# Attention of a two-block model: two heads at a time, matmuls in a fixed order

## The chip, the cores and the metric

The kernel runs on one core of a Trainium2 chip. The metric is the device time of one execution in microseconds. A core has a matrix engine (TensorE; its weight loads are listed apart, as PEld), VectorE (DVE), ScalarE (ACT), GpSimd (POOL) and a queue from which SyncE (SP) issues most loads. Matmul results land in PSUM, eight banks of 128 x 512 fp32 numbers; VectorE and ScalarE copy them on.

## What is computed

Two model blocks one after the other, 1024 tokens of width 1024. The change touches the attention of the second block only: two attentions of eight heads of width 64, cut into query blocks of 128.

```python
def forgetting_attention(q, k, v, log_f):          # "fox": own keys and values per head
    ...
        s = jnp.einsum('bqhd,bkhd->bhqk', q[:, start:end], k[:, :end], ...) * scale
        s = s + Ft[:, :, start:end, None] - Ft[:, :, None, :end]
        s = jnp.where(tk <= tq, s, -jnp.inf)
        p = jax.nn.softmax(s, axis=-1)
        outs.append(jnp.einsum('bhqk,bkhd->bqhd', p.astype(v.dtype), v[:, :end]))

def dsa_attention(q, k, v, qi, ki, wi):            # "dsa": one key and value head for all eight
    ...                                            # top-k choice of keys (here: an additive bias)
        s = jnp.einsum('bqhd,bqkd->bhqk', q[:, start:end], kg, ...) * scale
        p = jax.nn.softmax(s, axis=-1)
        outs.append(jnp.einsum('bhqk,bqkd->bqhd', p.astype(vg.dtype), vg))
```

## The kernel before

The program is written with tiles from pools; a planner orders each engine's instructions at build time by dependencies and modelled times, and each engine then runs its list in that order. `attention` (from L1530) comes after the projections of the second block and before `merge`, which multiplies the two attentions' outputs with their projection weights (L1715 loads them, L1726 to L1728 are its matmuls).

For a query block i (0 to 7) and a head, i+1 blocks of 128 keys take part, n = 128 (i+1) columns. `probs` (L1559) makes the scores: for each 512 columns a bank `pS` gets two matmuls (L1567 and L1570, fp32r, at least 256 columns wide), and in fox the last bank a third between them that adds the causal mask (L1569, bf16). VectorE adds the bias and keeps a running minimum (L1572), ScalarE takes the exponential and its row sum (L1574), both into the tile `S`. TensorE then transposes S block by block into a PSUM slot `pT` of up to four blocks (two such slots; L1624 in fox, L1657 in dsa), and `evac` (L1552) copies the slot to the tile `PT`, by ScalarE and VectorE in turn (L1555, L1557). The products with the values (L1629, L1661) accumulate over key blocks in the bank `po`: fp32 with 64 value columns as weights, the output in 64 of the 128 PSUM rows; each product is two records in the trace. After four query blocks (fox) or eight heads (dsa) `normalise` (L1577) inverts the row sums, spreads them by four matmuls (L1586) into a `pT` slot and scales `po`.

Fox runs over four pairs of heads (`hp2`), inside over the query blocks; a pair's two heads are in rows 0 to 63 and 64 to 127 of `po`, and the value products of the two heads take turns (L1627 to L1630). Its keys, queries and values are loaded per pair into one of two pools (`kps`), the row of forget sums `fr` into the first of them alone (L1598). Dsa (L1636 on) runs over the query blocks, inside over the eight heads, one after the other; heads 0 to 3 go to rows 0 to 63, heads 4 to 7 to rows 64 to 127. It has a pool of its own, `kp`, for its keys and two tiles of queries. Nothing ties TensorE to the written order: the planner mixes the kinds of matmul of different heads as they become ready.

Of the kernel before, what the change touches and what calls it, by code (L numbers as in the profile page):

```python
# [8 lines left out]
F32 = mybir.dt.float32  # L9
F32R = mybir.dt.float32r  # L10
# [3 lines left out]
AF = mybir.ActivationFunctionType  # L14
ALU = mybir.AluOpType
# [4 lines left out]
P = 128  # L20
D = 1024
NT = 8
# [1504 lines left out]
        self.es_h.close()  # L1527


def attention(B):  # L1530

    tc, dbg = B.tc, B.dbg
# [9 lines left out]
    with ExitStack() as e:  # L1542
        sp = e.enter_context(tc.tile_pool(name="b2s", bufs=3, reuse_waits="tile"))
        wk = e.enter_context(tc.tile_pool(name="b2ak", bufs=2, reuse_waits="tile"))
        kps = [e.enter_context(tc.tile_pool(name=f"b2k{j}", bufs=1, reuse_waits="tile")) for j in range(2)]
        kp = e.enter_context(tc.tile_pool(name="b2kd", bufs=2, reuse_waits="tile"))
        pss = e.enter_context(tc.tile_pool(name="b2pss", bufs=4, reuse_waits="tile", space=PSUM))
        pst = e.enter_context(tc.tile_pool(name="b2pst", bufs=2, reuse_waits="tile", space=PSUM))
        pso = e.enter_context(tc.tile_pool(name="b2pso", bufs=1, reuse_waits="tile", space=PSUM))
# [2 lines left out]
        def evac(dst, src):  # L1552
            flip[0] ^= 1
            if flip[0]:
                nc.scalar.copy(dst, src)  # L1555
            else:
                nc.vector.tensor_copy(dst, src)  # L1557

        def probs(q1, k1, k2, bias_ap, n, nm, diag, lsum):  # L1559

            S = sp.tile([P, 1024], F32, name=f"S{nm}", tag="S")
            mn = 3.0e38
            for lo in range(0, n, 512):
                pS = pss.tile([P, 512], F32, name=f"pS{nm}{lo}", tag="pS")
                w = min(512, n - lo)
                wm = max(256, w)
                nc.tensor.matmul(pS[:, :wm], q1, k1[:, lo:lo + wm], start=True, stop=False)  # L1567
                if diag and lo + 512 >= n:
                    nc.tensor.matmul(pS[:, w - P:w], identb, causb, start=False, stop=False)  # L1569
                nc.tensor.matmul(pS[:, :wm], q1, k2[:, lo:lo + wm], start=False, stop=True)  # L1570
                m = sp.tile([P, 1], F32, name=f"mn{nm}{lo}", tag="mn", bufs=8)
                nc.vector.tensor_tensor_reduce(S[:, lo:lo + w], pS[:, :w], bias_ap[:, lo:lo + w], 1.0, mn, ALU.add, ALU.min, m)  # L1572
                mn = m
            nc.scalar.activation(S[:, :n], S[:, :n], AF.Exp, bias=mn, scale=-1.0, accum_out=lsum)  # L1574
            return S

        def normalise(po, lsum, nm, cs, dh, dl):  # L1577

            rl = wk.tile([P, 2, 4], F32, name=f"rl{nm}", tag="rl")
            nc.vector.reciprocal(rl, lsum)  # L1580
            pr = pst.tile([P, 512], F32, name=f"prl{nm}", tag="pT")
            for j in range(4):
                rb = wk.tile([P, 2, 64], F32, name=f"rb{nm}{j}", tag="rlb", bufs=4)
                nc.vector.tensor_tensor(out=rb, in0=ones.rearrange("p (a b) -> p a b", a=2),
                                        in1=rl[:, :, j:j + 1].to_broadcast([P, 2, 64]), op=ALU.mult)
                nc.tensor.matmul(pr[:, j * P:(j + 1) * P], rb.rearrange("p a b -> p (a b)"), ident, start=True, stop=True)  # L1586
            rr = wk.tile([P, 512], F32, name=f"rr{nm}", tag="rr")
            nc.scalar.copy(rr, pr)
            nc.vector.tensor_tensor(out=rr, in0=rr, in1=po, op=ALU.mult)
            rv = rr.rearrange("p (a b) -> p a b", a=4)  # L1590
            nc.scalar.copy(dh, rv)
            nc.vector.tensor_tensor(out=dl, in0=rv, in1=dh.bitcast(F32), op=ALU.subtract)

        for hp2 in range(4):
            q1, k1, k2 = (kps[hp2 % 2].tile([P, 2, NT, P], F32R, name=f"{n}{hp2}", tag=n) for n in ("fq", "fk1", "fk2"))
            vt = kps[hp2 % 2].tile([P, NT, P], F32, name=f"fv{hp2}", tag="fvt")  # L1598
            fr = kps[0].tile([P, 2, 1024], F32, name=f"fr{hp2}", tag="fr")
            for half in range(2):  # L1600
                hs = slice(4 * half, 4 * half + 4)
                for dst, n in ((k1, "fk1"), (q1, "fq1"), (k2, "fk2")):
                    nc.sync.dma_start(dst[:, :, hs, :].bitcast(F32), st_d[n][:, 2 * hp2:2 * hp2 + 2, hs, :])
                if half == 0:
                    for q in range(2):
                        nc.sync.dma_start(fr[:, q, :], ft_d[2 * hp2 + q:2 * hp2 + q + 1, :].broadcast_to([P, 1024]))
                    nc.sync.dma_start(vt, fv_d[:, :, P * hp2:P * hp2 + P])
            for half in range(2):
                po = pso.tile([P, 512], F32, name=f"po{hp2}{half}", tag="po", bufs=2)
                ls = wk.tile([P, 2, 4], F32, name=f"ls{hp2}{half}", tag="ls")  # L1610
                for ii in range(4):
                    i = 4 * half + ii
                    n = (i + 1) * P
                    pts = []
                    for q in range(2):
                        nm = f"f{hp2}{i}{q}"
                        S = probs(q1[:, q, i, :], k1[:, q].rearrange("p t c -> p (t c)"),
                                  k2[:, q].rearrange("p t c -> p (t c)"), fr[:, q, :n], n, nm, True, ls[:, q, ii:ii + 1])
                        pT = sp.tile([P, 8, P], F32, name=f"PT{nm}", tag="PT", bufs=6)
                        for k0 in range(0, i + 1, 4):  # L1620
                            m = min(4, i + 1 - k0)
                            pp = pst.tile([P, 512], F32, name=f"pT{nm}{k0}", tag="pT")
                            for kk_ in range(m):
                                nc.tensor.transpose(pp[:, kk_ * P:(kk_ + 1) * P], S[:, (k0 + kk_) * P:(k0 + kk_ + 1) * P], ident)  # L1624
                            evac(pT[:, k0:k0 + m, :].rearrange("p a b -> p (a b)"), pp[:, :m * P])
                        pts.append(pT)
                    for kt in range(i + 1):  # L1627
                        for q in range(2):
                            nc.tensor.matmul(po[64 * q:64 * q + 64, ii * P:(ii + 1) * P], vt[:, kt, 64 * q:64 * q + 64],  # L1629
                                             pts[q][:, kt, :], start=(kt == 0), stop=(kt == i))  # L1630
                hs = slice(512 * half, 512 * half + 512)
                normalise(po, ls, f"f{hp2}{half}", hs, ofh[:, hp2, hs].rearrange("p (a b) -> p a b", a=4),
                          ofl[:, hp2, hs].rearrange("p (a b) -> p a b", a=4))


        dk1 = kp.tile([P, NT, P], F32R, name="dk1", bufs=1)  # L1636
        dk2 = kp.tile([P, NT, P], F32R, name="dk2", bufs=1)
        nc.sync.dma_start(dk1.bitcast(F32), dk_d[0])
        nc.sync.dma_start(dk2.bitcast(F32), dk_d[1])
        dk1 = dk1.rearrange("p t c -> p (t c)")  # L1640
        dk2 = dk2.rearrange("p t c -> p (t c)")
        for i in range(NT):
            n = (i + 1) * P
            q1 = kp.tile([P, 8, P], F32R, name=f"dq1_{i}", tag="dq1")
            nc.sync.dma_start(q1.bitcast(F32), dq_d[i])
            po = pso.tile([P, 512], F32, name=f"pod{i}", tag="po", bufs=2)
            ls = wk.tile([P, 2, 4], F32, name=f"lsd{i}", tag="ls")
            S = [None] * 8
            for h in range(8):
                S[h] = probs(  # L1650
                    q1[:, h, :], dk1, dk2, bias[i], n, f"d{i}{h}", False, ls[:, h // 4, h % 4:h % 4 + 1])
                pT = sp.tile([P, 8, P], F32, name=f"PTd{i}{h}", tag="PT", bufs=6)
                for k0 in range(0, i + 1, 4):
                    m = min(4, i + 1 - k0)
                    pp = pst.tile([P, 512], F32, name=f"pTd{i}{h}{k0}", tag="pT")
                    for kk_ in range(m):
                        nc.tensor.transpose(pp[:, kk_ * P:(kk_ + 1) * P], S[h][:, (k0 + kk_) * P:(k0 + kk_ + 1) * P], ident)  # L1657
                    evac(pT[:, k0:k0 + m, :].rearrange("p a b -> p (a b)"), pp[:, :m * P])
                q = h // 4
                for kt in range(i + 1):  # L1660
                    nc.tensor.matmul(po[64 * q:64 * q + 64, (h % 4) * P:(h % 4 + 1) * P], dvt[:, kt, :], pT[:, kt, :],  # L1661
                                     start=(kt == 0), stop=(kt == i))
            ts_ = slice(i * P, (i + 1) * P)
            normalise(po, ls, f"d{i}", None, odh[:, :, ts_], odl[:, :, ts_])
    B.es_a.close()
    B.of, B.od = (ofh, ofl), (odh, odl)
    if dbg and "of" in dbg:
# [586 lines left out]
```

## Time and profile before

| | us |
|---|---|
| median of three runs | 2946.06 (2944.88 to 2956.12) |
| the profiled execution | 2949.89 |
| its span, first to last instruction | 2948.1 |
| busy in the span: TensorE, weight loads | 2686.4 (91%), 2119.9 (72%) |
| busy: VectorE, ScalarE, GpSimd | 2128.3 (72%), 1484.9 (50%), 596.0 (20%) |
| mean granted clock of TensorE | 0.964 |

A busy share is the part of the span in which an engine has a record open; records of neighbouring matmuls overlap, so how fast matmuls follow each other is read from their starts. The granted clock is 1.00 at 2.4 GHz and 0.50 at 1.2 GHz; a stretch with both shows a mean.

### The profile page before, as it was taken

The numbers are of one execution on the slowest core, as the hardware profiler recorded it, in microseconds if no ns is written. First come the engines' busy times: TensorE is split into PE (matmuls) and PEld (weight loads), VectorE is DVE, ScalarE is ACT, GpSimd is POOL, SyncE is SP. The second block draws the span as 40 slices with busy tenths as digits, with TensorE's granted clock in tenths as the row PEclk, the third lists the DMA queues.
The fourth block names the chain that finished last, engine by engine and source line by source line (L and its number), as shares of the span: only waits on it lengthen the run. The fifth ranks groups of instructions, "written<-read, shape, count | busy, mean of one in ns | idle before, by whom it ended". The sixth has DMA issues, their size and how long they took to land. (4 is left out here: it accounts for less than half of the span.)

```text
span 2948.1 us, 39530 instructions
## 1 busy us (share of the span) xinstructions
PE 2686.4 (91%) x14016; PEld 2119.9 (72%) x14016; DVE 2128.3 (72%) x3664; ACT 1484.9 (50%) x2402; POOL 596.0 (20%) x449
## 2 busy tenths in 40 slices
PE   5999998999978897879999999999998799999997
PEld 2767776777757675658778777787777687777775
DVE  6776768876876567686676736654456899999996
ACT  4433334554532325557667535653122577777774
POOL 2000003333353214221222100000234212111112
PEclk9999999999989998899999999999999899999998
DMA  5255445654545232201322553002346799999995
GB/s 221 80 215 214 163 148 186 214 191 161 192 157 181 90 109 97 69 29 61 117 91 100 172 205 110 23 23 79 107 163 213 269 383 373 371 372 365 377 368 177
DMA packets 214180, 533.09 MB, mean 181 GB/s; under 512 B 25478, under 2 KB 70918, under 8 KB 209884
## 3 DMA queue, kind: packets, MB, share of 16 engines
q1 hardware_dynamic: 144768, 411.98, 39.3%
q10 hardware_dynamic: 57548, 84.99, 8.1%
q0 software_dynamic: 11664, 33.57, 4.6%
q8 instruction: 111, 1.82, 0.3%
q14 instruction: 89, 0.73, 0.1%
HBM read 449.25 MB, written 90.11 MB: 183 GB/s over the span
## 5 line engine op out<-in xcount | busy, mean ns | idle before, releaser
L2060 DVE TENSOR_TENSOR wh<-we,wh 128x1024 fp32r<-128x1024 f32 x390 | 456.3, 1219 | 15.5 <-ACT wh L2057 7.6
L2057 ACT CAST wh<-we 128x1024 fp32r<-128x1024 f32 x396 | 396.7, 1052 | 83.4 <-PE pye L2119 24.2
L450 DVE SCALAR_TENSOR_TENSOR acc<-img,cvw,acc 128x945 f32<-128x945 f32 (+2 forms) x160 | 193.1, 1219 | 53.8 <-ACT acc L441 51.8
L2096 PE MATMUL pae<-wh,xle 128*128 128x512 f32 x528 | 207.5, 394 | 5.9 <-DVE xle L2081 5.9
L2094 PE MATMUL pae<-wh,xhe 128*128 128x512 f32 x528 | 210.6, 399 | 2.2 <-ACT xhe L2080 2.2
L2095 PE MATMUL pae<-wh,xhe 128*128 128x512 f32 x528 | 209.9, 398 | 0.2 <-DVE wh L2060 0.2
L775 POOL TENSOR_TENSOR H<-H,expT 128x384 f32<-128x384 f32 x56 | 59.2, 1058 | 440.8 <-DMA H<-hs 349.7
L2117 PE MATMUL pye<-wh,ghe 128*128 128x512 f32 x264 | 107.4, 407 | 21.8 <-ACT ghe L2109 21.8
L2071 POOL DMA_INDIRECT xg<-h_d,gidx x33 | 35.9, 1089 | 448.5 <-PE pxe L2077 431.4
L2096 PEld LDWEIGHTS pae<-wh,xle 128*128 128x128 f32 x528 | 99.8, 189 | 27.0 <-DVE xle L2081 6.7
L2094 PEld LDWEIGHTS pae<-wh,xhe 128*128 128x128 f32 x528 | 100.0, 189 | 23.2 <-ACT xhe L2080 2.8
L2095 PEld LDWEIGHTS pae<-wh,xhe 128*128 128x128 f32 x528 | 100.0, 189 | 21.5 <-DVE wh L2060 1.4
L351 PE MATMUL pxz<-hTh,w_h 128*128 128x512 f32 x320 | 110.6, 413 | 3.0 <-ACT oz L705 2.4
L351 PE MATMUL pxc<-hTh,w_h 128*128 128x512 f32 x320 | 106.9, 408 | 5.1 <-ACT acc L441 5.1
L351 PE MATMUL pxz<-hTh,w_l 128*128 128x512 f32 x320 | 109.5, 412 | 0.0
L351 PE MATMUL pxz<-hTl,w_h 128*128 128x512 f32 x320 | 106.5, 407 | 0.0
L1751 POOL TENSOR_TENSOR sgl<-sgl 128x512 f32<-128x512 f32 x15 | 19.4, 1293 | 429.5 <-DMA wra<-in_w_pf 364.0
L768 POOL TENSOR_TENSOR xs<-xs,er 128x384 f32<-128x384 f32 x64 | 73.1, 1144 | 157.5 <-DVE er L766 140.5
L2119 PE MATMUL pye<-wh,gle 128*128 128x512 f32 x264 | 104.6, 396 | 0.1
L2118 PE MATMUL pye<-wh,ghe 128*128 128x512 f32 x264 | 103.4, 392 | 0.0
L1208 PE MATMUL ppg<-hg,h2Th 128*128 128x512 f32 x256 | 102.0, 400 | 0.6 <-ACT re L1360 0.6
L351 PE MATMUL pxc<-hTl,w_h 128*128 128x512 f32 x320 | 102.3, 397 | 0.0
(911 smaller groups left out, 7688.9 us busy)
## 6 DMA issues: line engine op xcount, KB each, us to landing
we<-in_w_ex SPq DMA_DIRECT2D x396, 512.0 KB
ad_w<-in_ada_w SPq DMA_DIRECT2D x24, 1024.0 KB
wr<-in_w_in SPq DMA_DIRECT2D x40, 512.0 KB
er<-ep_d SPq DMA_DIRECT2D x128, 96.0 KB
rbw<-pr_d SPq DMA_DIRECT2D x32, 384.0 KB
pf<-pr_d SPq DMA_DIRECT2D x32, 384.0 KB
xbc<-acc ACTq DMA_DIRECT2D x20, 512.0 KB
wada<-in_w_ada SPq DMA_DIRECT2D x8, 1024.0 KB
```

Of the source, the lines that this page charges most:

```text
L351: nc.tensor.matmul(px[j], wt[:, k, :mc], ht[:, k, 512 * j:512 * j + 512], start=(k == 0 and n == 0), stop=(k == KD - 1 and n == 2))
L450: nc.vector.scalar_tensor_tensor(o, img[:, r0 + dy:r1 + dy, c0 + dx:c1_ + dx], cvw[:, m, tap:tap + 1], o, op0=ALU.mult, op1=ALU.add)
L768: nc.gpsimd.tensor_tensor(out=y, in0=y, in1=er.rearrange("p (j t) -> p j t", j=3), op=ALU.add)
L1208: nc.tensor.matmul(pp, hTh[t][:, k, :], h, start=(k == 0), stop=False)
L2057: last["h"] = nc.scalar.copy(h, raw)
L2060: eng.tensor_tensor(out=l, in0=raw, in1=h.bitcast(F32), op=ALU.subtract)
L2094: nc.tensor.matmul(pa, xh[:, kk, :], h[:, cs], start=(kk == 0), stop=False)
L2095: nc.tensor.matmul(pa, xh[:, kk, :], l[:, cs], start=False, stop=False)
L2096: last["mm"] = nc.tensor.matmul(pa, xl[:, kk, :], h[:, cs], start=False, stop=(kk == KD - 1))
L2117: nc.tensor.matmul(o, gh[:, kk, :], h[:, cs], start=(kk == 0), stop=False)
L2118: nc.tensor.matmul(o, gh[:, kk, :], l[:, cs], start=False, stop=False)
L2119: nc.tensor.matmul(o, gl_[:, kk, :], h[:, cs], start=False, stop=(kk == 3))
```

## The change

Fox and dsa become generators of units: two heads and a query block. In dsa a unit holds heads j and j+4. For each unit all score matmuls of both heads are written first, the causal masks after them as the last matmul of their group. A step then writes the scores of one unit, the transposes of the unit two before it (`TLAG`) and the products of the unit before that: first up to four blocks of each head are transposed, into the two `pT` slots, then comes the first half of the products, in turns between the heads, then the other transposes and the rest of the products. `keep_in_program_order` ties these matmuls to this order on TensorE; VectorE, ScalarE and the loads are planned as before. `normalise` is split: the spreading matmuls come at the end of a later step. Buffers: S has six instead of three, PT five instead of six, the minimum twelve instead of eight, the row sums three instead of two; `fr` is in both pools; `kp` is gone, dsa's keys and queries lie in tiles of fox's size in `kps`, the queries two blocks to a tile. The copies of a unit's first head go to ScalarE and those of the second to VectorE, since the turns now go by head.

```diff
+TLAG = 2
+SBUFS = 6
...
-        kp = e.enter_context(tc.tile_pool(name="b2kd", bufs=2, reuse_waits="tile"))
...
-        def probs(q1, k1, k2, bias_ap, n, nm, diag, lsum):
...
+        queued = tc.keep_in_program_order
+
+        def scores(heads, n, nm, diag):
+
+            ps, res = [], []
+            for q, (q1, k1, k2, _, _) in enumerate(heads):
+                for lo in range(0, n, 512):
+                    pS = pss.tile([P, 512], F32, name=f"pS{nm}{q}{lo}", tag="pS")
+                    w = max(256, min(512, n - lo))
+                    last = diag and lo + 512 >= n
+                    queued(nc.tensor.matmul(pS[:, :w], q1, k1[:, lo:lo + w], start=True, stop=False))
+                    queued(nc.tensor.matmul(pS[:, :w], q1, k2[:, lo:lo + w], start=False, stop=not last))
+                    ps.append((q, lo, min(512, n - lo), pS))
+            if diag:
+                for q, lo, w, pS in ps:
+                    if lo + 512 >= n:
+                        queued(nc.tensor.matmul(pS[:, w - P:w], identb, causb, start=False, stop=True))
+            for q, (_, _, _, bias_ap, lsum) in enumerate(heads):
+                S = sp.tile([P, 1024], F32, name=f"S{nm}{q}", tag="S", bufs=SBUFS)
+                mn = 3.0e38
...
+                nc.scalar.activation(S[:, :n], S[:, :n], AF.Exp, bias=mn, scale=-1.0, accum_out=lsum)
+                res.append(S)
+            return res
+
+        def turned(Ss, i, nm, pts):
+
+            for q in range(2):
+                pts.append(sp.tile([P, 8, P], F32, name=f"PT{nm}{q}", tag="PT", bufs=5))
+            for k0 in range(0, i + 1, 4):
+                for q, (S, pT) in enumerate(zip(Ss, pts)):
+                    m = min(4, i + 1 - k0)
+                    pp = pst.tile([P, 512], F32, name=f"pT{nm}{q}{k0}", tag="pT")
+                    for kk_ in range(m):
+                        queued(nc.tensor.transpose(pp[:, kk_ * P:(kk_ + 1) * P], S[:, (k0 + kk_) * P:(k0 + kk_ + 1) * P], ident))
+                    evac(pT[:, k0:k0 + m, :].rearrange("p a b -> p (a b)"), pp[:, :m * P])
+                yield
+
...
+                queued(nc.tensor.matmul(pr[:, j * P:(j + 1) * P], rb.rearrange("p a b -> p (a b)"), ident, start=True, stop=True))
...
-        for hp2 in range(4):
-            fr = kps[0].tile([P, 2, 1024], F32, name=f"fr{hp2}", tag="fr")
...
+                q1, k1, k2 = (kps[hp2 % 2].tile([P, 2, NT, P], F32R, name=f"{n}{hp2}", tag=n) for n in ("fq", "fk1", "fk2"))
+                vt = kps[hp2 % 2].tile([P, NT, P], F32, name=f"fv{hp2}", tag="fvt")
+                fr = kps[hp2 % 2].tile([P, 2, 1024], F32, name=f"fr{hp2}", tag="fr")
...
-        dk1 = kp.tile([P, NT, P], F32R, name="dk1", bufs=1)
-        dk2 = kp.tile([P, NT, P], F32R, name="dk2", bufs=1)
...
-            for h in range(8):
-                S[h] = probs(
-                    q1[:, h, :], dk1, dk2, bias[i], n, f"d{i}{h}", False, ls[:, h // 4, h % 4:h % 4 + 1])
-                pT = sp.tile([P, 8, P], F32, name=f"PTd{i}{h}", tag="PT", bufs=6)
...
-                for kt in range(i + 1):
-                    nc.tensor.matmul(po[64 * q:64 * q + 64, (h % 4) * P:(h % 4 + 1) * P], dvt[:, kt, :], pT[:, kt, :],
-                                     start=(kt == 0), stop=(kt == i))
-            ts_ = slice(i * P, (i + 1) * P)
...
+                    for ii in range(4):
+                        i = 4 * half + ii
+                        n = (i + 1) * P
+                        heads = [(q1[:, q, i, :], k1[:, q].rearrange("p t c -> p (t c)"), k2[:, q].rearrange("p t c -> p (t c)"),
+                                  fr[:, q, :n], ls[:, q, ii:ii + 1]) for q in range(2)]
+                        yield (heads, i, f"f{hp2}{i}", True, lambda q, kt, vt=vt: vt[:, kt, 64 * q:64 * q + 64], po, ii, ls, to)
+
+        def dsa():
+            dks = kps[0].tile([P, 2, NT, P], F32R, name="dk", tag="fk1")
+            for j in range(2):
+                nc.sync.dma_start(dks[:, j].bitcast(F32), dk_d[j])
+            dk = [dks[:, j].rearrange("p t c -> p (t c)") for j in range(2)]
+            for i in range(NT):
+                n = (i + 1) * P
+                if i % 2 == 0:
+                    q2 = kps[i // 4].tile([P, 2, 8, P], F32R, name=f"dq1_{i}", tag=("fq", "fk2")[i // 2 % 2])
+                    for j in range(2):
+                        nc.sync.dma_start(q2[:, j].bitcast(F32), dq_d[i + j])
+                q1 = q2[:, i % 2]
+                po = pso.tile([P, 512], F32, name=f"pod{i}", tag="po", bufs=2)
+                ls = wk.tile([P, 2, 4], F32, name=f"lsd{i}", tag="ls", bufs=3)
+                ts_ = slice(i * P, (i + 1) * P)
+                for j in range(4):
+                    heads = [(q1[:, j + 4 * q, :], dk[0], dk[1], bias[i], ls[:, q, j:j + 1]) for q in range(2)]
+                    yield (heads, i, f"d{i}{j}", False, lambda q, kt: dvt[:, kt, :], po, j, ls, (odh[:, :, ts_], odl[:, :, ts_]))
+
+        def products(unit, pts):
+
+            _, i, _, _, values, po, ii, _, _ = unit
+            for kt in range(i + 1):
+                for q in range(2):
+                    queued(nc.tensor.matmul(po[64 * q:64 * q + 64, ii * P:(ii + 1) * P], values(q, kt), pts[q][:, kt, :],
+                                            start=(kt == 0), stop=(kt == i)))
+                if kt == i // 2:
+                    yield
+
+        scored, ready, sums = [], [], []
+
+        def step():
+
+            turns, done = iter(()), iter(())
+            if len(scored) > TLAG or (scored and not more):
+                unit, Ss = scored.pop(0)
+                pts = []
+                turns = turned(Ss, unit[1], unit[2], pts)
+                next(turns)
+                if ready:
+                    done = products(*ready[0])
+                ready.append((unit, pts))
+            elif ready and ready[0] is not None:
+                done = products(*ready[0])
+                ready.append(None)
+            next(done, None)
+            for _ in turns:
+                pass
+            for _ in done:
+                pass
+            for unit in sums:
+                normalise(unit[5], reciprocals(unit[7], unit[2]), *unit[8])
+            sums.clear()
+            if len(ready) > 1:
+                unit = ready.pop(0)[0]
+                if unit[6] == 3:
+                    sums.append(unit)
+
+        more = True
+        for unit in (u for f in (fox, dsa) for u in f()):
+            heads, i, nm, diag, _, _, _, _, _ = unit
+            scored.append((unit, scores(heads, (i + 1) * P, nm, diag)))
+            step()
+        more = False
+        while scored or ready[0] is not None or sums:
+            step()
```

## Rows read from the trace of the kernel before

**Rows 1.** Busy us (records) of PE, PEld, DVE, ACT, POOL; granted clock, DMA share, GB/s.

```profile
1724.00:1780.00 56.00, 50.85 (x366) 35.97 (x365) 28.63 (x97) 28.82 (x69) 0.00 (x0) 0.91 0.65 226
1780.00:2037.00 257.00, 255.48 (x1946) 200.68 (x1942) 155.11 (x497) 143.72 (x317) 0.00 (x0) 1.00 0.13 42
2037.00:2050.00 13.00, 10.09 (x38) 7.62 (x38) 5.50 (x7) 3.30 (x4) 0.00 (x0) 0.91 0.69 218
```

**Rows 2.** Waits (us in total, times, longest), and the load that was held.

```profile
SPq L1715 <- PE pSd L1570: 60.9, 1, 60.9
DVE Sf L1572 <- DMA fr<-ft_d: 5.8, 3, 3.8
2028.18 1.12 SPq L1715 DMA_DIRECT2D wra<-in_w_pf  x2
```

**Rows 3.** TensorE's timeline (start, duration, line, records): attention's start, its last products.

```profile
1731.30 0.70 PE L1629 MATMUL po<-PTf,fv 128*64 128x128 f32 x4 [2.12 <-DMA fv<-fv_d]
1731.92 0.69 PE L1624 MATMUL pTf<-ident,Sf 128*128 128x128 f32 x2
1732.54 0.69 PE L1629 MATMUL po<-PTf,fv 128*64 128x128 f32 x2
...
2035.53 1.09 PE L1661 MATMUL pod<-PTd,dvt 128*64 128x128 f32 x8
```

**Rows 4.** The same timeline inside fox.

```profile
1803.07 1.96 PE L1629 MATMUL po<-PTf,fv 128*64 128x128 f32 x30
1804.96 0.38 PE L1586 MATMUL prlf<-ident,rbf 128*128 128x128 f32 x1
...
1809.54 0.43 PE L1629 MATMUL po<-PTf,fv 128*64 128x128 f32 x2
1809.91 0.23 PE L1569 MATMUL pSf<-causb,identb 128*128 128x128 bf16 x1
```

**Rows 5.** The same timeline inside dsa.

```profile
1990.60 0.55 PE L1657 MATMUL pTd<-ident,Sd 128*128 128x128 f32 x3
1991.08 1.09 PE L1661 MATMUL pod<-PTd,dvt 128*64 128x128 f32 x8
1992.09 0.66 PE L1657 MATMUL pTd<-ident,Sd 128*128 128x128 f32 x4
...
2030.43 1.96 PE L1661 MATMUL pod<-PTd,dvt 128*64 128x128 f32 x16 [0.24 <-ACT PTd L1555]
2032.32 1.09 PE L1657 MATMUL pTd<-ident,Sd 128*128 128x128 f32 x8
```

**Rows 6.** The same timeline: scores of 256 and 512 columns, with masks and without.

```profile
1806.66 0.22 PE L1569 MATMUL pSf<-causb,identb 128*128 128x128 bf16 x1
1807.02 0.23 PE L1569 MATMUL pSf<-causb,identb 128*128 128x128 bf16 x1
...
1877.55 0.28 PE L1567 MATMUL pSd<-dk,dq 128*128 128x256 f32 x1
1877.67 0.28 PE L1570 MATMUL pSd<-dk,dq 128*128 128x256 f32 x1
...
2000.14 0.50 PE L1567 MATMUL pSd<-dk,dq 128*128 128x512 f32 x1
2000.48 0.40 PE L1570 MATMUL pSd<-dk,dq 128*128 128x512 f32 x1
2000.71 0.40 PE L1567 MATMUL pSd<-dk,dq 128*128 128x512 f32 x1
```

**Rows 7.** Durations: exponentials (min/median/max ns), then copies and reductions (busy us, mean ns).

```profile
L1574 ACT ACTIVATE Sf<-Sf,mnf x64: 387/777/1152, 1726.7 to 1869.6; 128x128 f32<-128x128 f32 x8, 128x256 f32<-128x256 f32 x8, 128x384 f32<-128x384 f32 x8, 128x512 f32<-128x512 f32 x8
...
L1555 ACT COPY PTd<-pTd 128x512 f32<-128x512 f32 x36 | 21.0, 583 | 31.0 <-PE pTd L1657 30.9
L1557 DVE COPY PTd<-pTd 128x512 f32<-128x512 f32 x12 | 8.3, 692 | 15.1 <-PE pTd L1657 15.1
L1572 DVE CUSTOM_DVE_ANT_0 Sd<-pSd,dbias 128x512 f32<-128x512 f32 x40 | 27.1, 682 | 4.9 <-PE pSd L1570 4.1 <-ACT PTd L1555 0.3
```

More of the change, by code (lines that the diff above doesn't have):

```diff
@@ L1557, in evac @@
                 nc.vector.tensor_copy(dst, src)
-        def probs(q1, k1, k2, bias_ap, n, nm, diag, lsum):
[L1561 to L1575, printed above, removed]
@@ L1577, in normalise @@
-        def normalise(po, lsum, nm, cs, dh, dl):
+        queued = tc.keep_in_program_order
[16 more added lines that the diff above has]
+                mn = 3.0e38
+                for _, lo, w, pS in (p for p in ps if p[0] == q):
+                    m = sp.tile([P, 1], F32, name=f"mn{nm}{q}{lo}", tag="mn", bufs=12)
+                    nc.vector.tensor_tensor_reduce(S[:, lo:lo + w], pS[:, :w], bias_ap[:, lo:lo + w], 1.0, mn, ALU.add, ALU.min, m)
+                    mn = m
+                nc.scalar.activation(S[:, :n], S[:, :n], AF.Exp, bias=mn, scale=-1.0, accum_out=lsum)
+                res.append(S)
+            return res
@@ L1579, in normalise, with reciprocals @@
+        def reciprocals(lsum, nm):
             rl = wk.tile([P, 2, 4], F32, name=f"rl{nm}", tag="rl")
@@ L1585, in normalise @@
                                         in1=rl[:, :, j:j + 1].to_broadcast([P, 2, 64]), op=ALU.mult)
-                nc.tensor.matmul(pr[:, j * P:(j + 1) * P], rb.rearrange("p a b -> p (a b)"), ident, start=True, stop=True)
+                queued(nc.tensor.matmul(pr[:, j * P:(j + 1) * P], rb.rearrange("p a b -> p (a b)"), ident, start=True, stop=True))
             rr = wk.tile([P, 512], F32, name=f"rr{nm}", tag="rr")
             nc.scalar.copy(rr, pr)
+            return rr
+        def normalise(po, rr, dh, dl):
             nc.vector.tensor_tensor(out=rr, in0=rr, in1=po, op=ALU.mult)
@@ L1592, in normalise @@
             nc.vector.tensor_tensor(out=dl, in0=rv, in1=dh.bitcast(F32), op=ALU.subtract)
-        for hp2 in range(4):
-            q1, k1, k2 = (kps[hp2 % 2].tile([P, 2, NT, P], F32R, name=f"{n}{hp2}", tag=n) for n in ("fq", "fk1", "fk2"))
-            vt = kps[hp2 % 2].tile([P, NT, P], F32, name=f"fv{hp2}", tag="fvt")
-            fr = kps[0].tile([P, 2, 1024], F32, name=f"fr{hp2}", tag="fr")
[L1600 to L1626, printed above, removed]
-                    for kt in range(i + 1):
-                        for q in range(2):
[L1629 to L1633, printed above, removed]
@@ new lines, in fox @@
+        def fox():
+            for hp2 in range(4):
+                q1, k1, k2 = (kps[hp2 % 2].tile([P, 2, NT, P], F32R, name=f"{n}{hp2}", tag=n) for n in ("fq", "fk1", "fk2"))
+                vt = kps[hp2 % 2].tile([P, NT, P], F32, name=f"fv{hp2}", tag="fvt")
+                fr = kps[hp2 % 2].tile([P, 2, 1024], F32, name=f"fr{hp2}", tag="fr")
+                for half in range(2):
+                    hs = slice(4 * half, 4 * half + 4)
+                    for dst, n in ((k1, "fk1"), (q1, "fq1"), (k2, "fk2")):
+                        nc.sync.dma_start(dst[:, :, hs, :].bitcast(F32), st_d[n][:, 2 * hp2:2 * hp2 + 2, hs, :])
+                    if half == 0:
+                        for q in range(2):
+                            nc.sync.dma_start(fr[:, q, :], ft_d[2 * hp2 + q:2 * hp2 + q + 1, :].broadcast_to([P, 1024]))
+                        nc.sync.dma_start(vt, fv_d[:, :, P * hp2:P * hp2 + P])
+                for half in range(2):
+                    po = pso.tile([P, 512], F32, name=f"po{hp2}{half}", tag="po", bufs=2)
+                    ls = wk.tile([P, 2, 4], F32, name=f"ls{hp2}{half}", tag="ls", bufs=3)
+                    hs = slice(512 * half, 512 * half + 512)
+                    to = [o[:, hp2, hs].rearrange("p (a b) -> p a b", a=4) for o in (ofh, ofl)]
+                    for ii in range(4):
[4 more added lines that the diff above has]
+                        yield (heads, i, f"f{hp2}{i}", True, lambda q, kt, vt=vt: vt[:, kt, 64 * q:64 * q + 64], po, ii, ls, to)
```

20 lines of the change are left out of this document (removed).

## The prediction, made from the kernel before alone

> **What bounds the kernel now.** I read the busy times by stretch first. From 1724 us, where the first score matmul starts, to 2037 us, where the output projection takes over, TensorE is busy 50.9 of 56 and 255.5 of 257 us; VectorE is busy 183.7 us of these 313 and ScalarE 172.5 [rows 1]. So attention costs what its matmuls cost on TensorE, and a wait elsewhere matters only where it reaches TensorE. The granted clock is 1.00 (2.4 GHz) but for the first 56 us (0.91). What follows hangs on attention: the weight loads of the output projection start at 2028.2 us, when the last score matmul has let their buffer go (a wait of 60.9 us on the load queue) [rows 2], and routing and experts come after. A shorter attention moves all of that forward.
>
> The second view is TensorE's timeline. A busy share hides what a matmul costs there, as records overlap; I take the distance from one start to the next, and call records of one kind without another between them a run. Between 1724 and 2037 us there are 551 runs, whose distances add up to 312.3 us: 62 runs of value products of the first half (fox) 48.6 us, 67 of the second (dsa) 71.4, 152 of transposes 71.7, 183 of scores 99.3, 64 causal masks 2.6, 23 of normalising matmuls 18.7. The first fox run and the last dsa run stand in [rows 3].
>
> **Prices, from single runs.** A value product is two records. Fox takes its two heads in turn, into the lower and the upper 64 columns of the array: 30 records from 1803.07 to 1804.96, 1.89 us, and 2 in 0.37 (1809.54 to 1809.91). That is 0.0545 us a record and 0.25 a run [rows 4]. Dsa takes one head after the other: 16 records from 2030.43 to 2032.32, also 1.89 us, and 8 in 1.01: 0.11 us a record and 0.15 a run [rows 5]. The same shape costs half where neighbours go to different columns. Three transposes between products take 0.48 (1990.60 to 1991.08): 0.11 each and 0.15 a run [rows 5]. Scores in a row step by 0.23 us (512 columns) and 0.12 (256), 384 between them at about 0.18; the first step after products is 0.34 instead of 0.23, so 0.11 a run. A mask and the score matmuls around it take 0.36 at 256 columns where two alone take 0.24, some 0.12; as a mask's own run is part of that, I take 0.10 [rows 6].
>
> **The change part by part.** No matmul is added or dropped: 1152 product records, 576 transposes, 384 scores, 64 masks. What changes is the neighbour.
>
> Dsa in pairs of heads j and j+4: their outputs lie in rows 0 to 63 and 64 to 127, as fox's do, and `products` takes them in turn. So dsa gets fox's price.
>
> Fixed order: a step is the scores of unit n, up to eight transposes of unit n-2, half the products of unit n-3, the other transposes (only where the block has more than four), the rest of the products. There are 64 units, 32 of them with a second run of transposes: 96 runs of products, 96 of transposes, 64 of scores, 16 of normalising matmuls.
>
> - Products: 1152 x 0.0545 + 96 x 0.25 = 87 us, before 120.0: -33. Of it -28 is dsa's pairing (71.4 to 44), -5 fox's fewer runs.
> - Transposes: 576 x 0.109 + 96 x 0.15 = 77 us, before 71.7: +5. Two thirds of the old runs ended in scores, which start early in a transpose; the new ones all end in products.
> - Scores: 192 x 0.23 + 128 x 0.12 + 64 x 0.18 + 64 x 0.11 = 78 us, masks 64 x 0.10 = 6, before 101.9: -18. The two masks of a unit now stand side by side, which no row shows; their price lies between 0 and 0.12, and I keep the nearest row's.
> - Normalising: 0; 16 runs instead of 23 may give some 2.
>
> The sum is **-46 us** (266 against 312), at full clock and with no wait. Waits must be added. In the first 56 us TensorE idled 5 us and the clock cost about 5 more (9% of 56). Score reductions waited 5.8 us for the row of forget sums [rows 2], which had one buffer; `fr` now has two, and its load no longer stands on the load queue behind the last reduction of the pair before. The rest of the start is data coming back from memory (2.1 us for the first values [rows 3]) and the slow clock after it, which stay: +5.
>
> New waits: TensorE keeps its order, so where a transpose waits, everything behind it waits. The tightest place is the second run of transposes: it needs the two PSUM slots that the first run filled. In the largest unit (8 blocks) slot one is full about 0.6 us after the run's start and its copy takes 0.58 on ScalarE, behind at most one exponential of 1.15 [rows 7]: 2.3 us. It is wanted after 8 x 0.109 + 0.15 + 0.25 + 16 x 0.0545 = 2.1 us, so a wait of 0 to 0.2. Slot two is wanted 0.44 later, and its VectorE copy takes 0.69. For all 64 units I take 4 us, between 0 and 32 x 0.2 + 0.5 for each of the 16 smallest units, whose steps are short, 14. VectorE now copies the second head of every unit, 288 of the 576 blocks of 128 columns instead of 240, at most 48 x 0.69 / 4 = 8 us more; 192 of some 274 us is 70% busy, so it stays hidden. Scores need four PSUM banks: the four reductions of the unit before take some 4 x 0.69 = 2.8 us [rows 7] of a large unit's 6.5 (8 x 0.23 + 0.11, 16 x 0.109 + 0.30, 32 x 0.0545 + 0.50, and 0.3 for normalising), so they are free.
>
> The tail: the last scores now come three steps (some 18 us) before the last product instead of 8 (2028.2 to the end of the last run [rows 2, 3]), and the projection's load buffers wait for them, so the weights are there earlier. Of the 2.9 us that TensorE idles from 2037 to 2050 [rows 1] I take -2. Dsa's keys and queries move into fox's buffers: the same two and eight loads on the same queue, the first with the last fox pair's work ahead of them (some 30 us), the last four free to go when fox ends, with only the projection's weights behind them: 0, and some 5 us once if the first came late.
>
> In all -46 + 5 + 4 - 2 = **-39 us**. The profiled execution took 2949.89 us (span 2948.1, 1.8 around it), 3.8 over the median of 2946.06; I put the change at the median: **2907 us**.
>
> **The rivals.** *B, waits at the slots.* The order costs 0.5 us more in each of the 32 large units, because a copy comes late: 2907 + 16 = 2923. For: both copying engines are in-order, and products waited 0.24 for a copy at 2030.43 [rows 5]. Against: the 2.1 us of cover.
>
> *C, no overlap in dsa.* Both heads use the same values as weights, which fox never shows. Then 576 x 0.0545 = 31 us less 48 x 0.10 for the cheaper run: +26, 2933, hardly to be told from no change. Against: fox's heads overlap although both use all 128 rows, and they have weight loads of their own [rows 4]. The Trainium skill (TensorE: Matmul & The Clock Gate, Part 3, The mechanism) says that a weight load overlaps a running matmul only where the row groups differ. By that rule the pairing gives nothing, as in C; the fox rows do not show it.
>
> *D, slower: each of the 96 runs of transposes waits for one exponential ahead of its copy*, 0.78 us in the median [rows 7]: 96 x 0.78 = 75, so 2982. It decides from 39/96 = 0.41 us a run. Against: TensorE idles under 2 us in 257 [rows 1]; copies wait for it.
>
> *E, slower: the clock falls in the longer runs of transposes.* At 1.2 GHz two transposes take 0.62 us, 0.31 each, where three take 0.48 at 2.4 [rows 3, 5]; 576 x 0.109 more is 63 us, 2970. Against: transposes take 71.7 of the 312 us, and the 257 us stand at 1.00 [rows 1]. The Trainium skill (same page, Part 4: PE-mode transpose) says that the full clock does not engage for transposes; these rows do not bear it out.
>
> **How the numbers follow.** A measurement of this kernel tells about 0.5% (15 us) from no change. Chances: forecast 0.68, own range 2890 to 2924; B 0.15; C 0.06; D 0.05; E 0.03; 0.03 for savings lost further on (between 2931 and 2946). Faster by over 0.5%: 0.68 + 0.15 + half of C = 0.86. Same: the other half of C and the last case, 0.06. Slower: 0.08. The low end, 2884, has no new wait (-4), masks at nothing (-6), start stalls gone (-5), fewer normalising and transposing runs' prices (-5) and a few us of rounding; the high end, 2934, takes in B and C.
>
> **What would show it.** In the profile after: dsa's product records step by 0.055 in pairs, in 48 runs, 32 records in some 2.0 us; attention is some 274 us long with TensorE idle under 12; VectorE is near 70% busy; no wait for the row of forget sums. The forecast is wrong if dsa's records still step by 0.11, if TensorE's idle time exceeds 30 us with a slot's copy as releaser, or if the clock is under 0.95 after the first 50 us.

## The result and the profile after

The changed kernel takes 2903.09 us (median of four runs, 2896.61 to 2908.41), the kernel before 2946.47 beside it: a ratio of 0.985, 95% interval 0.983 to 0.987. The forecast was 2907. In a later comparison on one chip (below) it took 2907.36 against 2944.37, a ratio of 0.987 (0.985 to 0.988). So the gain is 37 to 43 us.

The profiled execution of after has a span of 2904.9 us, 43.2 under that of before. First the busy times by stretch; the columns are those of [rows 1].

```profile
1720.00:1780.00 60.00, 53.50 (x418) 41.74 (x417) 33.73 (x115) 32.43 (x79) 0.00 (x0) 0.94 0.69 237
1780.00:1990.00 210.00, 202.32 (x1838) 161.70 (x1838) 154.82 (x478) 132.07 (x308) 0.00 (x0) 1.00 0.18 62
...
1725.70:1781.70 56.00, 49.50 (x411) 38.37 (x409) 35.29 (x120) 32.68 (x80) 0.00 (x0) 0.94 0.65 227
...
1725.70:1745.70 20.00, 13.89 (x89) 10.22 (x87) 9.90 (x39) 9.91 (x27) 0.00 (x0) 0.83 0.90 315
1998.00:2011.00 13.00, 13.00 (x60) 10.53 (x59) 4.64 (x7) 1.79 (x3) 2.08 (x2) 1.00 0.03 9
```

TensorE still sets the pace, 202.3 of 210 us busy at a granted clock of 1.00. The last row answers the third of [rows 1]: the output projection now starts without a gap. The third and fourth rows are attention's start, its first 56 and its first 20 us: in the latter TensorE is busy for 13.9 us, clock 0.83.

Attention, from the start of its first score matmul to the end of its last matmul, is 1725.7 to 1998.2, 272.4 us instead of 312.8: -40.4. It starts 1.5 later, and what follows it is 4.3 shorter in this execution. But in the later comparison the same kernel's execution had an attention of 271.8 us with 911.2 behind it, where before has 911.1 and the first execution of after 906.7. So what is shown is the 40 us inside attention; the 4 behind it are within what one execution differs from another, and so is the start (1718.7 in the execution of e1, below, whose edit lies behind it).

TensorE's time by kind, start to start as in the prediction, with what it idled in or right behind runs of that kind (the column of before leaves out, as the prediction did, its 24th run of normalising matmuls, 1.2 us, 0.7 of it idle):

| us | before | forecast, no wait | after | idle in it | rest |
|---|---|---|---|---|---|
| products | 120.0 | 87 | 89.1 | 10.1 | 79.0 |
| transposes | 71.7 | 77 | 82.6 | 4.1 | 78.5 |
| scores | 99.3 | 78 | 80.6 | 0.7 | 79.9 |
| masks | 2.6 | 6 | 5.2 | 0.9 | 4.3 |
| normalising | 18.7 | 18.7 | 14.7 | 0 | 14.7 |
| sum | 312.3 | 267 | 272.2 | 15.8 | 256.4 |

The steps themselves, from TensorE's timeline, as in [rows 3]: a fox step, fox's last products and dsa's first, then runs of dsa.

```profile
1850.24 1.04 PE L1599 MATMUL pTf<-ident,Sf 128*128 128x128 f32 x8
1851.21 0.88 PE L1678 MATMUL po<-PTf,fv 128*64 128x128 f32 x12
1852.02 0.83 PE L1599 MATMUL pTf<-ident,Sf 128*128 128x128 f32 x4
...
1863.51 1.97 PE L1678 MATMUL po<-PTf,fv 128*64 128x128 f32 x32
1865.41 0.39 PE L1572 MATMUL pSd<-dk,dq 128*128 128x256 f32 x1
...
1866.30 0.44 PE L1678 MATMUL pod<-PTd,dvt 128*64 128x128 f32 x4
1866.67 1.16 PE L1612 MATMUL prlf<-ident,rbf 128*128 128x128 f32 x8
...
1902.18 1.09 PE L1678 MATMUL pod<-PTd,dvt 128*64 128x128 f32 x16
1903.20 0.50 PE L1572 MATMUL pSd<-dk,dq 128*128 128x512 f32 x1
...
1905.69 0.66 PE L1678 MATMUL pod<-PTd,dvt 128*64 128x128 f32 x8
1906.73 0.56 PE L1599 MATMUL pTd<-ident,Sd 128*128 128x128 f32 x2 [0.38 <-ACT PTd L1558]
...
1973.61 1.09 PE L1599 MATMUL pTd<-ident,Sd 128*128 128x128 f32 x8 [0.23 <-ACT PTd L1558]
...
1981.19 1.09 PE L1599 MATMUL pTd<-ident,Sd 128*128 128x128 f32 x8 [1.72 <-ACT PTd L1558]
```

Sixteen dsa records take 1.02 us (1902.18 to 1903.20), where they took 1.89 [rows 5]; 32 in turns take 1.90 (1863.51 to 1865.41). The brackets are the new waits: TensorE at a second run of transposes, for ScalarE's copy of the first.

### The profile page after: what moved, and what is told of

The parts are those of the page before. It is cut to its first block, busy times and chain, and to the rows that moved or that the text cites. A ratio compares the mean times of both kernels' runs of the same rounds, so it can differ in the third digit from the quotient of the medians.

```text
span 2904.9 us, 39472 instructions
## 1 busy us (share of the span) xinstructions
PE 2634.7 (91%) x14016; PEld 2084.8 (72%) x14016; DVE 2133.9 (73%) x3664; ACT 1475.9 (51%) x2402; POOL 608.4 (21%) x449
## 5 line engine op out<-in xcount | busy, mean ns | idle before, releaser
L2177 POOL DMA_INDIRECT out_dram<-ye,gidx x33 | 97.7, 2960 | 76.3 <-DVE ye L2176 59.6
L351 PE MATMUL pxc<-hTh,w_l 128*128 128x512 f32 x320 | 102.0, 398 | 0.4 <-DVE w_l L144 0.4
```

Source lines behind the costliest of these rows:

```text
L351: nc.tensor.matmul(px[j], wt[:, k, :mc], ht[:, k, 512 * j:512 * j + 512], start=(k == 0 and n == 0), stop=(k == KD - 1 and n == 2))
L2177: nc.gpsimd.indirect_dma_start(out, bass.IndirectOffsetOnAxis(ap=gcol, axis=0), y, None, compute_op=ALU.add)
```

## The experiments

Each ratio is to the kernel before, run on the same chip; the kernel before took 2943.68 us beside the first four, 2949.04 beside the next four, and 2944.37 beside the last two. The sums by kind are made as in the table.

**e1_dsa_apart**: does the price of half need the alternation?

```diff
-            for kt in range(i + 1):
-                for q in range(2):
+            half = i // 2 + 1
+            for kts in (range(half), range(half, i + 1)):
+                pairs = [(kt, q) for kt in kts for q in range(2)] if unit[3] else [(kt, q) for q in range(2) for kt in kts]
+                for kt, q in pairs:
```

> The changed kernel, but in dsa the products of a half run go head after head (all key blocks of head j, then all of head j+4) instead of in turn; fox, the order of all other matmuls and the buffers stay. Theory (the two heads' products run side by side only when they alternate between the two halves of the columns): dsa's 576 product records go from 0.0545 to 0.109 us each, +31 us less what a few waits for copies give back (the products now cover the copies better, up to 6 us): dsa's product runs near 75 us instead of 46.8, the kernel at 2930 us (2925 to 2936), still faster than 2946 by the fewer runs. Rival (the gain is the fixed order and the fewer switches; heads side by side matter little): 2903 to 2910 us.

It took 2907.97 us, 0.988 (0.986 to 0.991), and dsa's products 51.0 us. The theory's reading, that neighbours must alternate, has fallen. Two of its runs of 16 records: the first is written as four records of one head, four of the other, and so once more; the second as eight and eight.

```profile
1887.74 1.15 PE L1680 MATMUL pod<-PTd,dvt 128*64 128x128 f32 x16
1888.81 1.16 PE L1612 MATMUL prld<-ident,rbd 128*128 128x128 f32 x8
...
1948.36 1.58 PE L1680 MATMUL pod<-PTd,dvt 128*64 128x128 f32 x16
1949.87 0.87 PE L1599 MATMUL pTd<-ident,Sd 128*128 128x128 f32 x6
```

They take 1.07 and 1.51 us; in turns it is 1.02. The starts of the second run's 16 records, in us:

```
1948.362 .522 .632 .741 .850 .856 .959 1949.016 .068 .125 .177 .234 .343 .452 .562 .671
```

Four stand alone, then come four pairs, then four alone again. Records do not name their half, but if the second head's eight were all held back behind the first's, no pair could be there. They read as the second head's stream setting in when the first has four records left. The record at .856 bears this out: it lasts 323 ns, as the run's first does and no other of the sixteen (272 or 273), and the starts go on from it as they do from the first, by 0.160 once and then by 0.109. By that reading the first run, with four at a time, overlaps from its first record on (its first two starts are 14 ns apart), and runs of 12 written as six and six should have two alone at either end: 8 x 0.109 + 0.15 = 1.02; ten of them take 1.07, with two alone at either end. So, as far as these runs show, the halves of the columns count, and TensorE reaches two products ahead; taking turns is one way to stay within that.

**e8_same_half**: the fixed order and the units kept, both heads of a dsa unit in the same rows of `po`, one head's products after the other's.

```diff
-                    heads = [(q1[:, j + 4 * q, :], ..., ls[:, q, j:j + 1]) for q in range(2)]
+                    heads = [(q1[:, h, :], ..., ls[:, h // 4, h % 4:h % 4 + 1]) for h in (2 * j, 2 * j + 1)]
...
+                    nc.tensor.matmul(po[64 * (h // 4):64 * (h // 4) + 64, h % 4 * P:(h % 4 + 1) * P], ...)
```

> The changed kernel, but a dsa unit holds heads 2j and 2j+1, whose outputs lie in the same 64 rows (the same half of the columns); the first half run is all products of one head, the second all of the other; order, buffers and fox as in the change. It comes after the run in which the heads of different halves stood head after head and dsa's product runs still took only 51.0 us. Theory, mended: what counts is that products for the two halves stand near each other in the queue, in whatever order; with both heads in one half nothing runs side by side: 576 x 0.109 + 47 x 0.15 = 70 us for dsa's runs plus some 2 us of waits, against 46.8: 2903 + 25 = 2928 us (2920 to 2934). Rival (the fixed order alone brings the gain, the halves do not matter): 2903 to 2908 us.

2928.48 us, 0.993 (0.991 to 0.996); dsa's products 70.7 us, 23.9 more than after. A run of it, and the groups of dsa's products by line, of this kernel and of after (busy us, mean ns | idle before):

```profile
1902.85 1.96 PE L1687 MATMUL pod<-PTd,dvt 128*64 128x128 f32 x16
1904.74 0.50 PE L1572 MATMUL pSd<-dk,dq 128*128 128x512 f32 x1
...
L1687 PE MATMUL pod<-PTd,dvt 128*64 128x128 f32 x576 | 72.9, 277 | 0.0
```

```profile
L1678 PE MATMUL pod<-PTd,dvt 128*64 128x128 f32 x576 | 42.5, 281 | 1.8 <-DVE PTd L1560 0.9 <-ACT PTd L1558 0.8
```

The weights and the order of kinds are those of after, but the half is not all that differs: each head's products also stand together, and in units of more than four blocks a run holds one head alone. The run shown is of a unit of four blocks: eight records of one head, then eight of the other, as in e1's second run. Its starts step by 0.109 throughout, 1.89 us against 1.51 there, and between these two runs only the half differs.

**e2_pairs_only**: the kernel before with dsa's heads in pairs j, j+4 and their products in turns, no fixed order.

```diff
-            for h in range(8):
+            for j in range(4):
+                for q in range(2):
+                    h = j + 4 * q
...
+                for kt in range(i + 1):
+                    for q in range(2):
+                        nc.tensor.matmul(po[64 * q:64 * q + 64, j * P:(j + 1) * P], dvt[:, kt, :], pts[q][:, kt, :], ...)
```

> The kernel before with one edit: dsa goes over pairs of heads j and j+4 as fox does, products in turn; the planner mixes the kinds as it likes, nothing is held in order, and the buffers are those of before. Theory: dsa's 67 product runs cost what fox's 62 cost in the same kernel, 48.6 instead of 71.4 us, so -23 us: 2923 us (2918 to 2930). The other 20 us of the change come from the order and the buffers. Rival A (pairing works only in a fixed order, because the planner breaks the pairs up): 2940 to 2946. Rival B (the fixed order adds nothing): 2903 to 2908.

2927.44 us, 0.994 (0.993 to 0.996). Attention is 294.4 us: dsa's products 49.5 us in 63 runs, scores with masks 103.7 (101.9 before), transposes 73.3. So pairing alone gives 16 us, the order and units without any overlap in dsa (e8) 21; together these are the 37 of the later comparison, where the first had 43.

**e3_none_between**: no products between the two runs of transposes.

```diff
-            next(done, None)
             for _ in turns:
                 pass
```

> The changed kernel, but without products between the two runs of transposes: a step is scores, all transposes of unit n-2, all products of unit n-3. Theory: 32 run pairs fewer (32 x 0.30 = -10 us), but the second transposes now want slot one at once. It is free some 0.58 us (its copy) to 1.7 us (an exponential of up to 1.15 ahead) after it is full, 0.44 us before the first run ends; so each of the 32 large units waits 0.3 to 1.3 us more, +10 to +42. In all 2903 to 2935, most likely 2918. TensorE's idle time before transposes rises from 4 + 10 us to 20 and more. Rival (the copies are hidden anyhow): 2893 us.

2926.31 us, 0.994 (0.992 to 0.996). Transposes take 114.0 us, 32.9 of them idle. Two of its second runs of transposes:

```profile
1943.08 0.70 PE L1599 MATMUL pTd<-ident,Sd 128*128 128x128 f32 x4 [1.21 <-ACT PTd L1558]
...
1956.45 0.73 PE L1599 MATMUL pTd<-ident,Sd 128*128 128x128 f32 x4 [1.22 <-ACT PTd L1558]
```

TensorE idles 38.4 us in attention, 22 more than in after: that is what the products between hide, and the time differs by about as much.

**e5_three_slots**: three PSUM slots for transposes, three banks for scores.

```diff
-name="b2pss", bufs=4
+name="b2pss", bufs=3
-name="b2pst", bufs=2
+name="b2pst", bufs=3
```

> The changed kernel with three PSUM slots for transposes instead of two and three banks for scores instead of four. Theory (TensorE waits for a slot's copy before the second transposes, about 6 to 7 us in all): with a third slot four of the eight second transposes start at once, the copies get 0.44 us more: -3 to -6 us; the fourth score bank of a large unit is wanted 1.4 us after the first, when the first reduction (0.69) has let its bank go: 0 to +3. In all 2897 to 2903. Rival (scores run into the reductions): 32 large units x 0.5 us, 2919.

2902.73 us, 0.985 (0.982 to 0.988): not to be told from after. The waits at the slots are nearly gone, and scores pay for it. From the groups by line, the transposes and the first score matmuls of dsa in this kernel, then in after:

```profile
L1599 PE MATMUL pTd<-ident,Sd 128*128 128x128 f32 x288 | 40.7, 276 | 1.2 <-ACT PTd L1558 1.2
L1572 PE MATMUL pSd<-dk,dq 128*128 128x512 f32 (+2 forms) x96 | 37.5, 398 | 0.7
```

```profile
L1599 PE MATMUL pTd<-ident,Sd 128*128 128x128 f32 x288 | 42.3, 278 | 6.7 <-ACT PTd L1558 6.2 <-ACT rrd L1614 0.2
L1572 PE MATMUL pSd<-dk,dq 128*128 128x512 f32 (+2 forms) x96 | 35.8, 381 | 0.0
```

Dsa's products fell from 46.8 to 38.7 us, transposes from 82.6 to 78.5, and scores rose from 80.6 to 88.6: of 12 us gained 8 were lost there, and attention is 3.5 shorter. The missing bank is the likely reason: the weight loads of the scores wait 17.2 us for VectorE's reductions, which empty these banks, where in after they wait 1.7.

**e4_one_fr**: the row of forget sums in one buffer again.

```diff
-                fr = kps[hp2 % 2].tile([P, 2, 1024], ...)
+                fr = kps[0].tile([P, 2, 1024], ...)
```

> The changed kernel, but the row of forget sums has one buffer again, as before. Theory: its load for a pair waits for the last reduction of the pair before and arrives some 3 us later, and the loads behind it on the queue wait too; the next pair's first reductions wait at each of the three pair changes, as in the kernel before (5.8 us there in three waits): +4 to +12 us, 2907 to 2915. Rival (the pipeline of three units rides over it): 2903.

2907.59 us, 0.988 (0.985 to 0.991), 4.5 over after's first figure and 0.2 over its second: the time does not settle it. The waits and TensorE's timeline do. First VectorE's wait in this kernel and where it reaches TensorE, then the wait in after:

```profile
DVE Sf L1584 <- DMA fr<-ft_d: 28.6, 5, 23.2
...
1761.96 1.09 PE L1599 MATMUL pTf<-ident,Sf 128*128 128x128 f32 x8 [1.00 <-ACT PTf L1558]
...
1795.69 1.09 PE L1599 MATMUL pTf<-ident,Sf 128*128 128x128 f32 x8 [1.43 <-ACT PTf L1558]
```

```profile
DVE Sf L1584 <- DMA fr<-ft_d: 25.4, 2, 24.5
```

The longest wait, in both, is VectorE's before the first reduction at all. The three more waits come with changes of head pair (1.3 to 1.8 us each), and behind each of them TensorE waits 1.00 to 1.43 at a second run of transposes, where after waits 0.22; its idle time in attention is 19.6 us instead of 15.9.

**e6_pools_swapped**: the two pools of loads exchanged, so that the first pair lies elsewhere.

```diff
+        kps = kps[::-1]
```

> The changed kernel with the two pools of keys, queries and values in swapped roles, so that the first pair's tiles lie elsewhere in memory. In the changed kernel the first query load was issued at 1719.6 us, held 17.7 us by the projection's last matmuls, whose memory its tile takes over; before it was issued at 1692.7. TensorE idles 6 us in the first 15 us of attention. Theory (that placement costs the start): loads go out earlier and 2 to 5 us come back, 2898 to 2901. Rival (the start waits for values and keys that the projection has just written): 2903.

2910.23 us, 0.987 (0.984 to 0.990), no gain: the theory has fallen. The first load was held still longer, by a projection matmul of the stage before (this kernel's row, then after's):

```profile
SPq L1637 <- PE ppfv L1210: 31.8, 1, 31.8
...
1733.69 0.55 PE L1573 MATMUL pSf<-fk,fq 128*128 128x256 f32 x1 [7.08 <-DMA fq<-fq_d]
```

```profile
SPq L1636 <- PE ppfv L1209: 17.7, 1, 17.7
```

TensorE then waits 7.08 us before attention instead of inside it: attention takes 267.8 us but starts at 1733.7.

**e7_copies_swapped** and **e9_dsa_swapped**: the first head's copies by VectorE and the second's by ScalarE, everywhere and in dsa alone. **e10_after_again**: the changed kernel beside e9.

```diff
-        flip = [0]
+        flip = [1]
```

```diff
         def dsa():
+            flip[0] += 1
```

> The changed kernel with the copies swapped: slot one (first head) by VectorE, slot two by ScalarE. In the changed kernel slot one's copy stands behind an exponential of up to 1.15 us on ScalarE, and TensorE waits some 0.4 us before the second transposes of most large dsa units. Theory (that wait): behind VectorE's reductions (0.69 to 0.75) slot one comes 0.3 us earlier and slot two, wanted 0.44 us later, bears the exponential: -2 to -5 us, 2898 to 2901. Rival (VectorE is the busier engine, its reductions of the running unit come first): +0 to +8 us.

> The changed kernel with ScalarE's and VectorE's copies exchanged in dsa alone (the first head of a pair goes to VectorE, the second to ScalarE). With the exchange everywhere, dsa's product runs fell from 46.8 to 42.2 us and fox's rose from 42.3 to 49.6. Theory: the two attentions are limited by different engines at that moment (ScalarE's exponentials in dsa, VectorE's reductions in fox), so the exchange in dsa alone keeps the gain: dsa's products 42 us, TensorE idle in attention 12 instead of 15.9, 2896 to 2900 us, 3 to 7 below the changed kernel. Rival: the gain in dsa came from the timing that fox left behind or is given back in dsa's transposes: 2901 to 2907.

> The changed kernel itself, beside the exchange in dsa alone, for a comparison on the same chip. 2903 us, between 2897 and 2909.

e7: 2907.87 us, 0.987 (0.984 to 0.990); dsa's products 42.2 us instead of 46.8, but fox's 49.6 instead of 42.3 and transposes 89.1 instead of 82.6. e9: 2905.41, 0.987 (0.985 to 0.988), against 2907.36 for after. The waits at dsa's slots in e9, then in after:

```profile
PE pTd L1599 <- ACT PTd L1558: 2.6, 4, 0.8
...
PE pTd L1599 <- DVE PTd L1560: 0.8, 3, 0.4
```

```profile
PE pTd L1599 <- ACT PTd L1558: 6.2, 13, 1.7
```

e9's attention takes 270.0 us, after's 271.8 beside it; dsa's products 42.8 and 46.1, transposes 83.3 and 82.1, TensorE's idle time 12.6 and 15.4. The waits fall as the theory had it, and a part comes back in the transposes, as the rival had it. The time lies in the rival's range, above the expected 2896 to 2900, and 2 us are too little for these runs to call it faster.

## Why the prediction was right, and where its steps were off

*Dsa in pairs* was right. The forecast was -28; the table's parts are 71.4 to 46.8, -24.6, with 6.8 of waits in it. e1 and e8 show the cause: of two runs written eight and eight only the one with its heads in different halves overlaps, and without any overlap (e8) dsa's products take 23.9 us more and the kernel's gain is 21 us.

*Rival C* has fallen, and the trace of before could have said so. Where it writes heads 3 and 4 one after the other, they go to different halves, and three of its 67 dsa runs step as e1's do. One of them has the starts of e1's run of eight and eight, again with a second record of 323 ns, the sixth:

```profile
1918.51 1.58 PE L1661 MATMUL pod<-PTd,dvt 128*64 128x128 f32 x16
1920.02 0.44 PE L1657 MATMUL pTd<-ident,Sd 128*128 128x128 f32 x2
```

The Trainium skill (TensorE: Matmul & The Clock Gate, Part 3, The mechanism) lets a weight load overlap a running matmul only where the row groups differ. All products here use 128 rows, and both heads have the same weights; still 16 records take 1.02 us in different halves and 1.89 in the same, and even in e8, in one half, weight loads are open for 61.6 of the 70.7 us of dsa's products. The measurement decides against the rule, for these matmuls. That the pairing then gains nothing was my step from it.

*The run price of products was mis-sized*: 0.25 us where after has 0.15 (4 records in 0.37, 32 in 1.90, so 0.0546 a record and 0.15 left). I took 0.25 from a fox run of 30 records in 1.89 [rows 4]. Those are 15 products, eight in one half and seven in the other, and the fuller half sets the time: 30 cost what 32 cost, and the last two of them start 0.109 apart, without a partner. The other row I used, 2 records in 0.37, is one product alone, likewise without a partner. Without waits products are 79.0 us, not 87.

*The new waits were mis-sized the other way*: outside the first 20 us TensorE idles 9.8 us (15.9 less 6.1), forecast 4. Of these 5.7 stand ahead of second runs of transposes, 1.9 within them, and 1.8 in attention's last products, which wait for their copies. The largest unit is not the tightest place, as I took it to be. With 16 records between two runs of transposes the wait ahead of the second is at most 0.23 (1973.61), about the 0 to 0.2 of my working; 1.72 once, at dsa's end, where the copy stood behind two exponentials. In dsa, units of five and six blocks and the first of seven have 8 or 12 records there to hide the same copy, and seven of these nine wait 0.28 to 0.41 (0.38 at 1906.73). In fox as many records leave no wait ahead of the second run, so their number is not all that decides. ScalarE shows what comes to it, in after:

```profile
1905.28 0.83 ACT L1586 ACTIVATE Sd<-Sd,mnd 128x640 f32<-128x640 f32 x1 [0.91 <-DVE mnd L1584]
...
1906.11 0.56 ACT L1558 COPY PTd<-pTd 128x512 f32<-128x512 f32 x1
```

The exponential begins just as the slot fills, and the copy goes behind it; it ends at 1906.67, and the transpose starts at 1906.73. This is *rival B*'s mechanism, at 5.7 us ahead of all second runs, where B asked for 16. *Rival D* asked for 0.78 us in each of 96 runs; even without products between (e3) transposes idle 32.9 us, not 75.

*Transposes*: +5 forecast, 77 us; without waits 78.5. *Scores with masks*: -18 forecast, -16.1 measured (101.9 to 85.8). The masks side by side take 5.2 us, forecast 6. *Normalising* was forecast at 0 and gave -4.0 by the table (-5.2 with the run that it leaves out): 16 runs of eight matmuls take 0.92 each, where 23 broken ones took 18.7.

*The start* did not improve. I put 5 us of loss there: TensorE idles 6.1 us in the first 20, and the clock of 0.83 costs some 2.4 more (17% of the 13.9 busy). Over the first 56 us, as the prediction counted, it is 6.5 idle and 3.4 for the clock of 0.94; before it was 5.2 and 5.0. The load of the first queries was held 17.7 us by a matmul of the projection, a wait that the prediction did not list among the changed buffers' effects; that its buffer now lies in that stage's memory is argued from e6, not shown. Nor is it shown that this hold cost anything: the first score matmul follows the projection's last one at once (1725.50, 1725.73), and of the 6.1 us 1.6 end with the first values, 2.7 with later queries, 1.2 with copies and 0.6 with a row of forget sums. E6 moved the idle time but did not remove it.

*The second buffer of `fr`*: the waits at the change of pair are gone, as forecast. The 24.5 us that stand against that row are VectorE's idle time before its first reduction. Before had them too, and the first reduction starts 1.0 us after the first score in both (first before, then after):

```profile
1725.28 0.29 DVE L1572 CUSTOM_DVE_ANT_0 Sf<-pSf,fr 128x128 f32<-128x128 f32 x1 [24.55 <-PE pSf L1570]
```

```profile
1726.73 0.29 DVE L1584 CUSTOM_DVE_ANT_0 Sf<-pSf,fr 128x128 f32<-128x128 f32 x1 [24.49 <-DMA fr<-ft_d]
```

What is left is one wait of 0.9 us for the other head's row, with 0.6 us of TensorE behind it.

*VectorE* is busy 67% (195.2 of 290 us), forecast 70.

*Rival E* did not come: the granted clock is 1.00 over the 210 us that hold nearly all runs of transposes.

*The tail*: -2 forecast. The gap ahead of the projection is gone ([rows 1] against 13.0 of 13), but what follows attention was 4.3 shorter in one execution and 0.2 longer in another, so no size is shown.

In all the forecast matmul time was 267 us and is 256 with 2.4 of slow clock in it, 13 less at full clock; the start took 3.5 of that back (8.5 for 5) and the new waits 5.8 (9.8 for 4). That 2907 came within 4 us of the time is in part luck, as these errors lie on both sides. Of the signs set down beforehand one did not come: TensorE idles 15.9 us in attention, not under 12. What stays open is the size of e4's and e9's effects on the time, and whether the two products that TensorE reaches ahead in e1 hold for other shapes.

## What to carry to other kernels

Value products that fill 64 columns should be written so that near neighbours go to different halves of the array, with as many for one half as for the other in each run; price a run from rows where that is so. Where TensorE's order is fixed, look for the tightest wait in every size of unit, as the work that hides a copy may shrink faster than the copy, and at what its engine runs ahead of the copy. A PSUM bank taken from another use may only move the wait.

## What was not expected of the hardware

Matmuls to the other half of the columns run ahead of earlier-written ones, by about four records: dsa's products cost 51.0 us written head after head, 46.8 in turns (with 4.5 us more of waits) and 70.7 in one half. The Trainium skill (TensorE: Matmul & The Clock Gate, Part 3, The mechanism) states that matmuls start and end strictly in written order; the starts listed under e1 do not agree, as far as the halves can be inferred from them and from the two records of 323 ns.
